# A new order at the head of a long kernel: parameters on another DMA queue, x in four transfers, a split first weight, squares moved back

## The chip, the core and the metric

The kernel runs on one core of a Trainium2 chip. Its time is the device time of one execution in microseconds (us); 1663.65 us is the median of three runs of the kernel before (1662.88 to 1664.98). TensorE (PE) does the matrix products, VectorE (DVE) and ScalarE (ACT) the elementwise work, GpSimd (POOL) almost nothing but small transfers, and SyncE (SP) issues nearly all DMA transfers.

## The reference

Two blocks on 256 tokens of width 1024, all in float32. The first block puts 16 meta tokens in front of x (272 rows) and runs two layers. What the change touches is the head of layer 0:

```
h    = concatenate([meta_tokens, x])                       # 272 x 1024
hn   = h * rsqrt(mean(h*h, axis=-1) + 1e-5) * norm1_g[l]    # first norm
proj = hn @ w_in[l]                                        # 1024 x 2560: q, k, v, u
a, gate = split(u + b_glu[l])
z    = a * sigmoid(gate)                                   # then conv, attention, MLP
```

After the two layers comes a second block: modulated norm, a gated delta rule in chunks, dilated attention, and a mixture of 64 experts of which each token takes 8.

## The kernel before, in words

**Tiling.** Activations lie transposed, 128 of the 1024 features on the partitions and the 272 tokens along the row, so h is eight tiles of 128 x 272. x arrives with tokens on the partitions and is turned by PE: for each of the eight feature blocks three transposes (L320, L322) and one copy out of PSUM by DVE (L323). The meta tokens are in `bigb`, x in `biga`.

**Weights.** A weight tile is 1024 x 256 float32 (1 MB), loaded by `weights` (L158) into one of three buffers `raw`. ACT rounds it in two halves to a high part `hi` (L165), DVE takes the rest as low part `lo` (L166). A product is three matmuls: high by high, high by low of the activations, low by high (L172, L173, L174). The first norm's activations are split in the same way: `xh` by ACT (L268), already times the norm's gain, and `xl` by DVE (L269).

**First norm.** Because the token's scale can be put on afterwards, the products don't wait for it. ACT squares each h tile (L273), PE adds the squares up over the features with a matrix of ones (L274, each in two passes), ACT takes the root (L201) and DVE the reciprocal `rstd` (L202). The results of the first two weight tiles, `a` and `g`, are multiplied by it on the way out of PSUM (L359, L360). Those PSUM tiles are `mm`, of which there are three, and `ax`, also three, one of which holds the sum of squares. The third weight tile needs two more `mm` tiles, so its second half waits until DVE has read the first tile of the first weight, which it can't do before `rstd` is there.

**Parameters.** `columns` (L204) loads rows of parameters and turns them with one transpose into columns. PE does this for norm1_g and b_glu (tile `pv_norm_g`) ahead of all transposes of x.

**What sets the order.** The program is written with tiles and no explicit order between engines; a scheduler works out at build time what stands where in each engine's queue, by a model of the timeline. `high_priority(offset=n)` lets what stands inside count as if it were written n places earlier. Each engine then runs its queue strictly in order. Transfers issued by SP and ACT take eight completion semaphores in turn, and a transfer waits until the earlier holder of its semaphore has landed. POOL issues its own transfers (lam_q, lam_k and other small parameters) with eight of their own; each lam vector is read 128 times, once for each partition.

Of the kernel before, what the change touches and what calls it, by code (L numbers as in the profile page):

```python
# [15 lines left out]
NM, S, D = 16, 256, 1024  # L16
T = NM + S
# [82 lines left out]
def dap(src, off, dims):  # L100
    return bass.AP(tensor=src.tensor, offset=src.offset + off, ap=dims)
# [8 lines left out]
class K:  # L110
    def __init__(s, ctx, tc, I, out, dbg):
        s.ctx, s.tc, s.nc, s.I, s.out, s.dbg = ctx, tc, tc.nc, I, out, dbg
        nc = tc.nc
        s.nraw, s.nhi, s.late = 3, 3, False
        s.V, s.A, s.PE, s.G, s.SP = nc.vector, nc.scalar, nc.tensor, nc.gpsimd, nc.sync
        s.cp = ctx.enter_context(tc.tile_pool(name="cp", bufs=1))
        s.wp = ctx.enter_context(tc.tile_pool(name="wp", bufs=1))
        s.hp = ctx.enter_context(tc.tile_pool(name="hp", bufs=1))
        s.bp_ = [ctx.enter_context(ExitStack()) for _ in range(2)]
        s.bp = [e.enter_context(tc.tile_pool(name="bp" + n, bufs=1, side=n, reuse_waits="tile"))  # L120
                for e, n in zip(s.bp_, ("left", "right"))]
        s.xp = {}
        s.pp_ = ctx.enter_context(ExitStack())
        s.pp = s.pp_.enter_context(tc.tile_pool(name="pp", bufs=1, space=bass.MemoryType.PSUM))
# [28 lines left out]
    def weights(s, src, r0, nk, c0, split=True, ld=None):  # L153

        with s.tc.high_priority(offset=PRI):
            ld = ld or src.ap[-2][0]
            raw = s.wp.tile([128, 8, 256], F32, name="raw", bufs=s.nraw)
            s.SP.dma_start(raw[:, :nk], dap(src, r0 * ld + c0, [[ld, 128], [128 * ld, nk], [1, 256]]))  # L158
            if not split:
                return raw  # L160
            hi = s.wp.tile([128, 8, 256], F32R, name="hi", bufs=s.nhi)
            lo = s.wp.tile([128, 8, 256], F32R, name="lo", bufs=s.nhi)
            h2 = (nk + 1) // 2
            for a, b in ((0, h2), (h2, nk)):
                s.A.copy(hi[:, a:b], raw[:, a:b])  # L165
                s.V.tensor_tensor(lo[:, a:b], raw[:, a:b], hi[:, a:b].bitcast(F32), op=OP.subtract)  # L166
            return hi, lo
# [89 lines left out]
            s.moe()  # L257


    def norm_in(s, h, g, t0, n):  # L260

        ap, A, V = s.ap, s.A, s.V
        xh = ap.tile([128, KC, T], F32R, name="xh")
        xl = ap.tile([128, KC, T], F32R, name="xl")
        ss = s.ax()
        sl = slice(t0, t0 + n)
        for k in range(KC):
            A.activation(xh[:, k, sl], h[:, k, sl], AF.Copy, scale=g[:, k:k + 1])  # L268
            V.scalar_tensor_tensor(xl[:, k, sl], h[:, k, sl], g[:, k:k + 1], xh[:, k, sl].bitcast(F32),  # L269
                                   op0=OP.mult, op1=OP.subtract)  # L270
            sq = ap.tile([128, T], F32, name="sq", bufs=3)
            with s.tc.high_priority(offset=200):
                A.activation(sq[:, :n], h[:, k, sl], AF.Square)  # L273
                s.PE.matmul(ss[:, :n], s.C["ones"], sq[:, :n], start=(k == 0), stop=(k == KC - 1))  # L274
        r = ap.tile([128, T], F32, name="rstd", bufs=2)
        with s.tc.high_priority(offset=200):
            s.rsqrt(r[:, sl], ss[:, :n], s.eps5, 1.0 / D)
        return (xh, xl), r

# [26 lines left out]
    def first_block(s):  # L306
        nc, I, V, A, PE, SP, ap, cp = s.nc, s.I, s.V, s.A, s.PE, s.SP, s.ap, s.cp
        C, ident = dict(s.C), s.C["ident"]
        xin = s.big(0, F32, (2, D))
        xm = s.big(1, F32, (D,))[:NM]  # L310
        with s.tc.high_priority(offset=FIRST):
            for o in range(0, D, D // 2):
                SP.dma_start(xin[:, :, o:o + D // 2], dap(I["x"], o, [[D, 128], [128 * D, 2], [1, D // 2]]))
            SP.dma_start(xm, I["meta_tokens"])
            P = s.columns(ap, ap, (("norm1_g", 16), ("b_glu", 16)), SP, tag="scr", bufs=3)
        h = s.hp.tile([128, KC, T], F32, name="h", bufs=2)
        for k in range(KC):
            p = s.ax()
# [8 lines left out]
        for l in range(2):  # L327
            w_in = I["w_in"][l]
            tq = NM if l else 0
            nq = T - tq  # L330
            x, r = s.norm_in(h, P["norm1_g"][:, 8 * l:8 * l + 8], 0, T)
            if l == 0:
                C.update(s.consts(ap, 1))
                hbg = ap.tile([128, 2, 4], F32, name="hbg")
                for i in range(2):
                    V.tensor_scalar(hbg[:, i], P["b_glu"][:, 8 * i + 4:8 * i + 8], 0.5, None, op0=OP.mult)
            s1 = s.big(0)
# [12 lines left out]
            for b in range(2):  # L350
# [4 lines left out]
                for j in range(2):  # L355
# [5 lines left out]
                    A.activation(g1, g1, AF.Tanh, bias=hbg[:, l, c:c + 1], scale=0.5)  # L361
                    A.activation(a1, a1, AF.Identity, bias=P["b_glu"][:, 8 * l + c:8 * l + c + 1])
                    V.scalar_tensor_tensor(z[:, c, CW - 1:], g1, 1.0, a1, op0=OP.add, op1=OP.mult)
# [6 lines left out]
            for i, (t0, n) in enumerate(((tq, nq), (0, T))):  # L370
# [3 lines left out]
                for b in range(2):  # L374
                    w = s.weights(w_in, 0, 8, 512 * i + 256 * b)
                    for j, p in enumerate(s.block2([(w, 8, 0)], x, t0, n)):
                        raw = ap.tile([128, T], F32, name="qraw", bufs=2)
# [9 lines left out]
            if l == 0:  # L387
                P.update(s.columns(ap, ap, (("norm2_g", 16), ("conv_b", 8), ("conv_ln_g", 8), ("conv_ln_b", 8),
                                            ("subln_g", 2)), s.G, tag="scr", bufs=3))
# [3 lines left out]
                for i in range(2):  # L393
                    V.tensor_scalar(subg[:, i:i + 1], P["subln_g"][:, i:i + 1], 1.0 - LAM0[i], None, op0=OP.mult)
                V.tensor_scalar(hlg, P["conv_ln_g"], 0.5, None, op0=OP.mult)
                V.tensor_scalar(hlb, P["conv_ln_b"], 0.5, None, op0=OP.mult)
# [178 lines left out]
            x, r = s.norm_in(h1, P["norm2_g"][:, 8 * l:8 * l + 8], tq, nq)  # L575
# [17 lines left out]
            h = s.hp.tile([128, KC, T], F32, name="h", bufs=2)  # L593
# [1134 lines left out]
```

## Time and profile before

| | us |
|---|---|
| median of three runs | 1663.65 |
| the profiled execution | 1670.4 |
| its span, first to last instruction | 1668.6 |
| PE busy in the span | 1603.3 |
| DVE busy | 862.3 |
| ACT busy | 757.1 |

The profile is of one execution, 6.75 us longer than the median; 1.8 us of it lie outside the span. "Busy" of PE counts overlapped instructions as well, so 96% is a sign of few gaps, not of a full array. The chain that ended last is 83% PE, 7% DMA (mostly the experts' weights near the end), 5% ACT and 3% DVE. The first 13 us of the span hold no PE instruction at all.

### The profile page before, as it was taken

The numbers are of one execution on the slowest core, as the hardware profiler recorded it, in microseconds if no ns is written. First come the engines' busy times: TensorE is split into PE (matmuls) and PEld (weight loads), VectorE is DVE, ScalarE is ACT, GpSimd is POOL, SyncE is SP. The second block draws the span as 40 slices with busy tenths as digits, with TensorE's granted clock in tenths as the row PEclk, the third lists the DMA queues.
The fourth block names the chain that finished last, engine by engine and source line by source line (L and its number), as shares of the span: only waits on it lengthen the run. The fifth ranks groups of instructions, "written<-read, shape, count | busy, mean of one in ns | idle before, by whom it ended". The sixth has DMA issues, their size and how long they took to land.

```text
span 1668.6 us, 32896 instructions
## 1 busy us (share of the span) xinstructions
PE 1603.3 (96%) x13616; PEld 1358.8 (81%) x13616; DVE 862.3 (52%) x1763; ACT 757.1 (45%) x1548; POOL 14.5 (1%) x28
## 2 busy tenths in 40 slices
PE   6998999999999999998999999999899999999997
PEld 6965999999967999988999899999666576556563
DVE  5685766646986666448655654554322221222122
ACT  5375644435437544455855866743322221222221
POOL 2000000000000000000000000000000000000000
PEclk9999999999988999999999999999999999999999
DMA  8408555555455555653333333556799999999995
GB/s 240 149 26 266 194 179 174 172 178 168 136 177 172 182 189 184 215 191 122 126 128 102 102 128 102 192 192 226 314 380 420 421 419 420 420 419 420 421 419 245
DMA packets 209958, 389.29 MB, mean 233 GB/s; under 512 B 8854, under 2 KB 183312, under 8 KB 184976
## 3 DMA queue, kind: packets, MB, share of 16 engines
q1 hardware_dynamic: 209104, 386.66, 63.1%
q8 instruction: 108, 1.77, 0.4%
q0 software_dynamic: 704, 0.51, 0.3%
q14 instruction: 42, 0.34, 0.1%
HBM read 386.10 MB, written 1.05 MB: 232 GB/s over the span
## 4 chain that ended last, share of the span: by engine, by line
PE 83%; DMA 7%; ACT 5%; DVE 3%; issue 1%; SPq 0%; ACTq 0%; DVEq 0%
PE mm L172 14%; PE mm L174 14%; PE mm L173 14%; PE pm L1542 9%; PE pm L1568 5%; DMA we<-in_w_exp_up 5%; PE pm L1505 3%; PE dx L486 2%; PE mm L195 1%; PE mm L196 1%; PE mm L197 1%; PE dx L628 1%; PE mm L459 1%; PE acc L1586 1%; ACT hi L165 1%; PE ax L274 1%
## 5 line engine op out<-in xcount | busy, mean ns | idle before, releaser
L166 DVE TENSOR_TENSOR lo<-raw,hi 128x1024 fp32r<-128x1024 f32 (+2 forms) x300 | 347.8, 1191 | 144.7 <-ACT hi L165 143.5
L165 ACT CAST hi<-raw 128x1024 fp32r<-128x1024 f32 (+2 forms) x300 | 292.7, 1024 | 267.6 <-PE mm L173 154.0
L172 PE MATMUL mm<-xh,hi 128*128 128x272 f32 (+1 forms) x1008 | 288.1, 288 | 0.0
L173 PE MATMUL mm<-xl,hi 128*128 128x272 f32 (+1 forms) x1008 | 287.8, 286 | 0.0
L174 PE MATMUL mm<-xh,lo 128*128 128x272 f32 (+1 forms) x1008 | 286.6, 286 | 0.0
L1542 PE MATMUL pm<-we,xT 128*32 128x256 f32 (+2 forms) x2048 | 194.2, 389 | 6.3 <-DMA we<-in_w_exp_up 5.5
L173 PEld LDWEIGHTS mm<-xl,hi 128*128 128x128 f32 x1008 | 189.7, 188 | 0.9
L174 PEld LDWEIGHTS mm<-xh,lo 128*128 128x128 f32 x1008 | 189.3, 188 | 0.5
L172 PEld LDWEIGHTS mm<-xh,hi 128*128 128x128 f32 x1008 | 188.5, 188 | 0.8
L1542 PEld LDWEIGHTS pm<-we,xT 128*32 128x32 f32 (+2 forms) x2048 | 123.1, 129 | 72.6 <-DMA we<-in_w_exp_up 7.8
L173 PE MATMUL mm<-bigb,hi 128*128 128x256 f32 (+1 forms) x512 | 148.6, 291 | 0.0
L172 PE MATMUL mm<-hh,hi 128*128 128x256 f32 x384 | 110.5, 291 | 7.3 <-ACT hh L702 4.2
L1568 PE MATMUL pm<-we,hT 128*32 128x512 f32 (+2 forms) x512 | 114.8, 599 | 0.4 <-DMA we<-in_w_exp_down 0.3
L173 PE MATMUL mm<-hl,hi 128*128 128x256 f32 x384 | 109.6, 286 | 0.7 <-DVE hl L703 0.7
L174 PE MATMUL mm<-hh,lo 128*128 128x256 f32 x384 | 108.6, 286 | 0.0
L1553 DVE SCALAR_TENSOR_TENSOR hp<-sil,cs,pm 128x256 f32<-128x256 f32 x26 | 17.6, 676 | 164.8 <-ACT sil L1551 164.8
L174 PE MATMUL mm<-biga,lo 128*128 128x272 f32 (+1 forms) x352 | 101.4, 288 | 0.0
L172 PE MATMUL mm<-biga,hi 128*128 128x272 f32 (+1 forms) x352 | 100.6, 286 | 0.0
L173 PEld LDWEIGHTS mm<-bigb,hi 128*128 128x128 f32 x512 | 97.9, 191 | 0.5
L1573 DVE TENSOR_TENSOR y<-pm,gt 128x512 f32<-128x512 f32 x52 | 35.8, 689 | 107.4 <-PE pm L1568 107.4
L195 PE MATMUL mm<-hi,hh 128*128 128x256 f32 x288 | 86.0, 299 | 2.0 <-DVE cacc L859 2.0
L1551 ACT ACTIVATE sil<-pm 128x256 f32<-128x256 f32 x26 | 10.0, 385 | 170.2 <-PE pm L1542 170.2
(544 smaller groups left out, 3102.7 us busy)
## 6 DMA issues: line engine op xcount, KB each, us to landing
we<-in_w_exp_gate SPq DMA_DIRECT2D x64, 1024.0 KB, 18.2
we<-in_w_exp_up SPq DMA_DIRECT2D x64, 1024.0 KB, 19.5
we<-in_w_exp_down SPq DMA_DIRECT2D x64, 1024.0 KB, 17.7
raw<-in_w_in SPq DMA_DIRECT2D x62, 1024.0 KB, 5.0
raw<-in_w_gate_up SPq DMA_DIRECT2D x44, 1024.0 KB, 5.0
raw<-in_w_ada SPq DMA_DIRECT2D x22, 1024.0 KB, 6.2
raw<-in_w_down SPq DMA_DIRECT2D x16, 1024.0 KB, 5.1
raw<-in_w_out SPq DMA_DIRECT2D x12, 1024.0 KB, 5.4
```

Source lines behind the costliest of these rows:

```text
L165: s.A.copy(hi[:, a:b], raw[:, a:b])
L166: s.V.tensor_tensor(lo[:, a:b], raw[:, a:b], hi[:, a:b].bitcast(F32), op=OP.subtract)
L172: s.PE.matmul(ps[:, :n], a, xh, start=start, stop=False)
L173: s.PE.matmul(ps[:, :n], a, xl, start=False, stop=False)
L174: s.PE.matmul(ps[:, :n], b, xh, start=False, stop=stop)
L195: s.PE.matmul(p[:, :256], xh, w[0][:, k], start=(k == 0), stop=False)
L486: PE.matmul(p[:, :nq], dg, z[:, c, tq + j:tq + j + nq], start=(j == 0), stop=(j == n - 1))
L1505: s.PE.matmul(p[:, 256 * kk:256 * kk + 256], s.ht[h][:, i, k + kk], oh[:, i], start=(i == 0 and h == 0), stop=(i == 1 and h == 1))
L1542: mm = PE.matmul(gu[sg, 256 * m:256 * m + 256], xT[:, k, o + sg.start:o + sg.stop], w[m][:, k], start=(k == 0), stop=(k == 7))
L1553: V.scalar_tensor_tensor(hp.rearrange("p k q -> p q k"), sil.rearrange("p (q k) -> p q k", k=2), cs, gu[:, 256:].rearrange("p (q k) -> p q ...
L1568: PE.matmul(py[sg], hT[:, k, sg], w[2][:, k, 512 * j:512 * j + 512], start=(k == 0), stop=(k == 1))
L1573: V.tensor_tensor(y, py, s.gt2[:, 512 * j:512 * j + 512], op=OP.mult)
```

## The change

It does four things at the head of the kernel. The two transfers of norm1_g and b_glu are issued from ACT's queue and no longer from SP's, and are written ahead of x. x comes in four transfers of 256 columns in place of two of 512, with the meta tokens behind the first of them. The first weight tile comes in two transfers of four row blocks each. In layer 0 the squares, their sums and the reciprocal root get priority offset -200 in place of 200, so they count as written later. Nothing else is edited, but since the scheduler works the whole program out anew, the order changes in later places too, among them the second block.

```diff
-        s.nraw, s.nhi, s.late = 3, 3, False
+        s.nraw, s.nhi, s.late, s.first = 3, 3, False, True
...
-            s.SP.dma_start(raw[:, :nk], dap(src, r0 * ld + c0, [[ld, 128], [128 * ld, nk], [1, 256]]))
+
+            for a, b in ((0, 4), (4, 8)) if s.first else ((0, nk),):
+                s.SP.dma_start(raw[:, a:b], dap(src, (r0 + 128 * a) * ld + c0, [[ld, 128], [128 * ld, b - a], [1, 256]]))
+            s.first = False
...
-    def norm_in(s, h, g, t0, n):
+    def norm_in(s, h, g, t0, n, first=200):
...
-            with s.tc.high_priority(offset=200):
+            with s.tc.high_priority(offset=first):
                 A.activation(sq[:, :n], h[:, k, sl], AF.Square)
                 s.PE.matmul(ss[:, :n], s.C["ones"], sq[:, :n], start=(k == 0), stop=(k == KC - 1))
         r = ap.tile([128, T], F32, name="rstd", bufs=2)
-        with s.tc.high_priority(offset=200):
+        with s.tc.high_priority(offset=first):
             s.rsqrt(r[:, sl], ss[:, :n], s.eps5, 1.0 / D)
...
-            for o in range(0, D, D // 2):
-                SP.dma_start(xin[:, :, o:o + D // 2], dap(I["x"], o, [[D, 128], [128 * D, 2], [1, D // 2]]))
-            SP.dma_start(xm, I["meta_tokens"])
-            P = s.columns(ap, ap, (("norm1_g", 16), ("b_glu", 16)), SP, tag="scr", bufs=3)
+            P = s.columns(ap, ap, (("norm1_g", 16), ("b_glu", 16)), A, tag="scr", bufs=3)
+            for o in range(0, D, D // 4):
+                SP.dma_start(xin[:, :, o:o + D // 4], dap(I["x"], o, [[D, 128], [128 * D, 2], [1, D // 4]]))
+                if o == 0:
+                    SP.dma_start(xm, I["meta_tokens"])
...
-            x, r = s.norm_in(h, P["norm1_g"][:, 8 * l:8 * l + 8], 0, T)
+            x, r = s.norm_in(h, P["norm1_g"][:, 8 * l:8 * l + 8], 0, T, 200 if l else -200)
```

Lines below the edits stand three or four numbers higher in the changed kernel (L274 is L277 there, L172 is L175).

The start of SP's queue, before:

```order
1 L150 DMA blob_73<-in_blob 128x384
2 L313 DMA biga<-in_x 128x2x512 x2
3 L314 DMA bigb<-in_meta_tokens 16x1024
4 L210 DMA pv_norm_g<-in_norm_g 16x128
5 L210 DMA pv_norm_g<-in_b_glu 16x128
6 L158 DMA raw<-in_w_in 128x8x256 x3
7 L150 DMA blob_181<-in_blob 128x944
```

and after (the blob is a table of constants, the identity for the transposes among them):

```order
1 L150 DMA blob_73<-in_blob 128x384
2 L317 DMA biga<-in_x 128x2x256
3 L319 DMA bigb<-in_meta_tokens 16x1024
4 L317 DMA biga<-in_x 128x2x256 x3
5 L160 DMA raw<-in_w_in 128x4x256
6 L160 DMA raw<-in_w_in 128x8x256
7 L160 DMA raw<-in_w_in 128x4x256
8 L160 DMA raw<-in_w_in 128x8x256
9 L150 DMA blob_183<-in_blob 128x944
```

The second half of the first weight has moved behind the second weight, and the two parameter transfers are gone from here; they are the first two rows of ACT's queue now.

PE around the last of the eight sums of squares, with what each row waits for. Before, it lies inside the second weight tile (which writes `ax`), and the first matmul that waits for DVE to free an `mm` tile comes fifty rows later, at row 139:

```order
86 L274 MATMUL ax<-sq,blob_73 128x272 [waits Activation_49]
87 L173 MATMUL ax<-xl,hi 128x272
88 L174 MATMUL ax<-xh,lo 128x272
89 L274 MATMUL ax<-sq,blob_73 128x272 [waits Activation_49]
90 L172 MATMUL ax<-xh,hi 128x272
91 L173 MATMUL ax<-xl,hi 128x272
```

After, it stands at the end of the first half of the third weight tile:

```order
144 L175 MATMUL mm<-xh,hi 128x272
145 L176 MATMUL mm<-xl,hi 128x272
146 L177 MATMUL mm<-xh,lo 128x272
147 L277 MATMUL ax<-sq,blob_73 128x272
148 L175 MATMUL mm<-xh,hi 128x272 [waits DVE_49]
149 L176 MATMUL mm<-xl,hi 128x272
```

The matmul that needs a freed `mm` tile is now the very next one. Between the first weight and row 147 PE does 120 weight matmuls; before row 139 it did 115.

On ACT the root of that norm (L201 before, L204 after) stands behind the high parts of weights four and five, where before it stood between them. The four CASTs ahead of it are these two weights:

```order
18 L168 CAST hi<-raw 128x1024 x3
19 L302 ACTIVATE lsum<-lsum 128x4
20 L168 CAST hi<-raw 128x1024 x4
21 L204 ACT_TABLE_LOAD
22 L204 ACTIVATE rstd<-ax,eps_75 128x272
```

Further down, where the second block's delta rule and dilated attention are interleaved, ACT has 55 table loads in all in place of 51. No edit touches these lines.

## Rows read from the trace of the kernel before

**Rows 1.** The page's head and its engines' busy time.
```profile
span 1668.6 us, 32896 instructions
PE 1603.3 (96%) x13616; PEld 1358.8 (81%) x13616; DVE 862.3 (52%) x1763; ACT 757.1 (45%) x1548; POOL 14.5 (1%) x28
```
**Rows 2.** Waits, first 30 us: who waited for what, us in total, times, longest.
```profile
PE ax L214 <- DMA pv_norm_g<-in_b_glu: 13.1, 1, 13.1
```
**Rows 3.** Timeline of SP's queue (6.54 also alone): start us, duration, what, count.
```profile
0.76 0.39 SPq L150 DMA_DIRECT2D blob<-in_blob  x1
1.20 0.94 SPq L313 DMA_DIRECT2D biga<-in_x  x2
3.15 1.17 SPq L210 DMA_DIRECT2D pv_norm_g<-in_b_glu  x1
4.36 8.65 SPq L158 DMA_DIRECT2D raw<-in_w_in  x3
...
6.54 6.47 SPq L158 DMA_DIRECT2D raw<-in_w_in  x1
...
22.71 0.38 SPq L158 DMA_DIRECT2D raw<-in_w_in  x1
```
**Rows 4.** DMA issues of single stretches: KB each, median us from issue to landing.
```profile
blob<-in_blob SPq DMA_DIRECT2D x1, 192.0 KB, 2.5
pv_norm_g<-in_b_glu SPq DMA_DIRECT2D x1, 8.0 KB, 9.8
raw<-in_w_in SPq DMA_DIRECT2D x1, 1024.0 KB, 11.8
raw<-in_w_in SPq DMA_DIRECT2D x1, 1024.0 KB, 4.9
```
**Rows 5.** The tile views of biga (x) and raw, first 30 us: all landings.
```profile
DMA to landing us min/median/max: 4.8/7.0/9.1
...
DMA to landing us min/median/max: 4.9/9.5/15.7
```
**Rows 6.** Timeline of POOL: its issues held until a lam transfer has landed.
```profile
7.42 0.50 POOL L210 DMA_DIRECT2D pv_norm_g<-in_subln_g  x1 [1.88 <-DMA lamv<-in_lam_q]
13.00 0.51 POOL L210 DMA_DIRECT2D pv_b_ada<-in_g_mix  x1 [0.93 <-DMA lamv<-in_lam_k]
```
**Rows 7.** Timeline of PE: first transposes, squares, first product, third weight.
```profile
13.15 0.26 PE L320 MATMUL ax<-blob,bigb 16*128 16x16 f32 x1
13.96 0.28 PE L320 MATMUL ax<-blob,bigb 16*128 16x16 f32 x1
19.66 2.27 PE L274 MATMUL ax<-sq,blob 128*128 128x272 f32 x6
21.56 0.49 PE L172 MATMUL mm<-xh,hi 128*128 128x272 f32 x1
38.33 0.42 PE L172 MATMUL mm<-xh,hi 128*128 128x272 f32 x2
```
**Rows 8.** The chain of waits, pieces of PE: start, us.
```profile
24.43 0.46 PE ax L274 x2
...
27.39 0.25 PE mm L172 x2
```
**Rows 9.** Timeline of DVE and ACT around weights and the first norm.
```profile
16.96 1.98 ACT L165 CAST hi<-raw 128x1024 fp32r<-128x1024 f32 x2
20.39 2.29 DVE L166 TENSOR_TENSOR lo<-raw,hi 128x1024 fp32r<-128x1024 f32 x2
31.73 1.28 ACT L201 ACT_TABLE_LOAD   x1
33.03 0.49 ACT L201 ACTIVATE rstd<-ax,eps 128x272 f32<-128x272 f32 x1
33.55 1.85 DVE L202 RECIPROCAL rstd<-rstd 128x272 f32<-128x272 f32 x1 [0.39 <-ACT rstd L201]
35.44 0.79 DVE L359 TENSOR_TENSOR a<-mm,rstd 128x272 f32<-128x272 f32 x2
```
**Rows 10.** Windows: us, PE busy, PEld, DVE, ACT, POOL, granted clock, DMA, GB/s.
```profile
30.00:40.00 10.00, 10.00 (x79) 9.84 (x78) 8.66 (x11) 7.33 (x9) 1.34 (x3) 1.00 0.93 290
820.00:845.00 25.00, 24.68 (x247) 23.91 (x246) 18.80 (x41) 22.00 (x56) 1.38 (x1) 1.00 0.36 118
915.00:945.00 30.00, 27.00 (x222) 25.81 (x220) 17.28 (x34) 27.50 (x75) 0.00 (x0) 1.00 0.31 100
```
**Rows 11.** Waits of PE, 915 to 975 us.
```profile
PE dx L1121 <- ACT dpT L1116: 1.7, 1, 1.7
PE dx L1083 <- DVE dtk L1080: 1.3, 1, 1.3
```

## The prediction

> **What bounds the kernel now.** I read the page's head first: PE is busy 1603.3 of 1668.6 us [rows 1], so some 65 us of gaps are all that a change of order can win, and a shift at the head is worth its full length later if PE has no gap behind it. The waits of the first 30 us come next: the longest wait of PE in the whole run is one of 13.1 us for the transfer of b_glu [rows 2]. The reader is to see that this is an 8 KB transfer, issued at 3.15 [rows 3] and landed 9.8 us later [rows 4]. It stood sixth in SP's queue behind all of x. The landings say why the queue is slow: the second half of x was issued at about 1.67 (half of the 0.94 us behind 1.20 [rows 3]) and took 9.1 us, the first half only 4.8 [rows 5]. In the same time POOL's four lam transfers run; the first has landed by 7.42 and the last by 13.00 [rows 6]. I take it that they share the DMA engines with x and that the slowest engine sets when a transfer counts as landed.
>
> From 13.05 PE is a chain: eight blocks of transposes, 0.81 us apart (13.15 to 13.96), squares from 19.66, the first product at 21.56 [rows 7]. From there PE has no gap (10.00 of 10 us in 30 to 40, at granted clock 1.00 [rows 10]). So what counts is when the first products start, and whether PE then runs on.
>
> **The change, part by part.** Its profiled execution took 1670.4 us (span 1668.6 and 1.8 around it), 6.75 more than the median of the runs; I work out differences in that execution and take them off the median.
>
> *Parameters on ACT's queue.* Two issues leave SP's queue and stand first on ACT's, ahead of a table load that nothing needs before h exists. A transfer of 192 KB that is first in its queue lands in 2.5 us [rows 4]; one behind x lands at 13.0. I take the near end, about 3.3, because nothing stands before them now. The cover is x itself: if they land any time before the first quarter of x, they cost nothing.
>
> By the Trainium skill (DMA: Bandwidth & Descriptors, "Issuing engines are not separate DMA queues") transfers started by ScalarE and SyncE run on the same 16 engines and interleave, so that another issuer saves only issue time. Taken at its word, the parameters would land as late as before; that is the slow rival below. That b_glu took four times as long as the 24 times larger constants agrees with a shared engine and with a queue alike; no run so far tells them apart.
>
> *x in four.* Twice the issues (about 0.47 us each, hidden, since the data take longer than the issues). The first quarter lands between 3.3 and the 6.0 of the old half (1.20 + 4.8), I take 4.7. The last lands between 6.0 and the old 10.8 (1.67 + 9.1); of the four lam transfers one now runs ahead of the others, which POOL issues some 2.5 us later, so I take 8.5, the middle. Then two blocks of transposes (1.6) and three sums of squares (1.9, from 19.66 to 21.56 [rows 7]) end at 12.0. Here the transposes are off the path.
>
> *First weight in two.* What is late next is the weights. The first landed at about 16.2 (4.36 + 11.8 [rows 3, 4]), the third at 22.2 (6.54 [rows 3] + the longest landing, 15.7 [rows 5]), so some 3 us a weight. The half weight can land no sooner than 0.5 MB behind x, about 10, and no later than 14.6 (half a step before the old first). Nothing is taken off the DMA engines' work, so I stay near the late end: 13.6, the second weight at 16.7, the second half at 18.3, the third at 21.3. One cast (0.99, half of 1.98 [rows 9]) makes the first product start at 14.7 in place of 21.56. These 6.9 us would be the gain if PE ran on.
>
> *Squares behind the high parts.* This takes much of it back. The last sum of squares is now PE's 147th row, directly ahead of a matmul that needs `rstd`; between them lie the root (0.49), the reciprocal (1.85) and the first product with it (0.44, by the pair's 0.79) [rows 9], 2.8 us in which PE's queue stands. Before, the sum was long done and nothing waited. Two ways lead there:
> - PE's own: 14.7, then 120 products at 0.125 and five sums at 0.46 [rows 8], 15.0 + 2.3, and 1.2 us where the fourth and fifth sum wait for ACT, which squares them behind a cast: 33.2. With the 2.8 us: 36.0.
> - ACT's: its root is now queued behind the casts of weights four and five. The fourth is issued when DVE has the low part of the first weight's second half: landing 18.3, squares and casts ahead on ACT to 20.8, low part 1.15 (half of 2.29 [rows 9]): 22.0, hardly earlier than the 22.71 of before [rows 3]. It lands 4.9 later [rows 4], at 27.0; the fifth, issued with it, at 29.5 to 31.9 (none to one full latency further), I take 29.7. Two casts 1.98, table load 1.28, then the 2.8 us: 35.8.
>
> Before, PE had the same work behind it (115 products at 38.45, five more at 0.125) at 39.1 [rows 7, 8]. So the head gains 39.1 - 36.0 = 3.1 us.
>
> *TensorE's speed.* The first squares came at 0.32 us a pass, later ones at 0.23 [rows 7, 8], though the granted clock of that stretch is not recorded lower. If the first 24 products run at half rate too, they cost up to 3.0 us more; most of that lies in the waits for ACT. I take 0.3, leaving 2.8.
>
> *Later order.* The scheduler's new order brings four more table loads on ACT in the second block, 1.28 each [rows 9]: 5.1 us. ACT is busy 22.00 of 25 and 27.50 of 30 us there [rows 10], but PE waits for ACT or for DVE behind it only now and then (1.7 and 1.3 are the two longest in 60 us [rows 11]). Between 0 and 5.1 I take a quarter, 1.3. That other swaps there gain or lose a microsecond or two can't be read off.
>
> The Trainium skill (ScalarE: Activation LUTs, "What ACT_TABLE_LOAD costs") has 2.66 us for each switch, load and drain; four would be 10.6. The trace shows the root starting 0.02 us behind the load's end (31.73 + 1.28 against 33.03 [rows 9]), so I stay with 1.28.
>
> Sum: -2.8 + 1.3 = -1.5 us, 1663.65 - 1.5 = 1662.1, or 1668.9 for a profiled execution.
>
> **The rivals.**
> - *The weights come much earlier (chance 0.25).* If the lam transfers, later now, no longer hold up the slowest engine, the half weight lands at 10 and the products start at 11. PE's way is then 11 + 18.5 + 2.8 = 32.3; ACT's shifts by the same 3.7 if the low parts keep pace, to 32.1. Gain 6.8, less 0 to 1.3: about 1657.5. For it: the first x half took 4.8 us with one lam transfer in flight. Against it: the same bytes and the same lam transfers still run before 13 us.
> - *The squares come too late for a head that gains little (0.08).* If the parameters land at 13.0 as before, everything up to the first product stays at 21.56, and from there 15.0 + 2.3 + 2.8 make 41.7, which is 2.6 us behind the old 39.1; with the table loads +3.9: 1667.5. The wait of row 148 decides it, and the point is a first product at 17.8: later than that, the head loses. It is the page's rule on issuing engines that would bring this about. Against it: b_glu waited in one queue behind a megabyte.
> - *The table loads all lie on the path (0.12).* +5.1 against -2.8: 1665.9. For it speaks ACT's busy share, against it that PE's named waits there are short.
> - *The transfers gain nothing (0.05).* Four small ones on the same busy engines land as late as two, and the half weight at 14.6 or later: then 1663.5.
>
> **How the numbers follow.** My forecast, 1662.1, has 0.50 with a range of its own from 1659.5 to 1664.5 (weights one microsecond either way, 0 to 3 for the table loads). 0.2% is 3.3 us, about what a measurement of this kernel can tell from no change. Faster than 1660.3 are nearly all of the first rival and a fifth of the forecast: 0.36. Slower than 1667.0 are most of the second rival and part of the third, with swaps in the second block against us: 0.13. The rest, 0.51, is within. The range goes from 1656.5, the first rival without table loads, to 1667.5.
>
> **What would show it.** In the new profile: the transfer of b_glu landing before 5; the first transpose before 6 and the last before 11; the first product between 13 and 16; ACT's root at 32 to 34; and a gap of PE of 2 to 3 us before a product of the third weight, released by DVE's first read of `mm`, at about 36. If PE has no such gap, the squares' price was wrong and the kernel is faster than I say. If the first transpose is still at 13, the queue was not the cause. If the head has gained 3 us at 40 and the end has not, the second block took it, and the two stretches of [rows 10] will show ACT fuller and PE's waits longer.

## The result, and the profile after

The changed kernel takes 1679.95 us (four runs, 1678.99 to 1680.72), the kernel before 1663.27 beside it (four runs, 1662.31 to 1664.98): 1.0099 times as long, 95% interval 1.0081 to 1.0116. That is 16.7 us slower, outside the predicted range. The traced execution took 1680.7 us.

The page's head and its engines' busy time, to be laid beside [rows 1]:

```profile
span 1678.8 us, 32882 instructions
PE 1611.1 (96%) x13616; PEld 1365.4 (81%) x13616; DVE 862.9 (51%) x1763; ACT 762.2 (45%) x1552; POOL 14.5 (1%) x28
```

PE has the same number of matmuls and is busy 7.8 us longer, so part of its work ran slower; the span grew by 10.2, so its gaps grew too. ACT has four instructions more, the four table loads.

PE's waits in the first 50 us (compare [rows 2]), and PE's timeline at the first transpose, the first product, the first product that waits for the root and the products behind it (compare [rows 7]):

```profile
PE ax L217 <- DMA pv_norm_g<-in_b_glu: 4.1, 1, 4.1
PE mm L175 <- DVE a L363: 3.0, 1, 3.0
PE ax L324 <- DMA bigb<-in_meta_tokens: 2.9, 1, 2.9
```
```profile
7.24 0.28 PE L324 MATMUL ax<-blob,bigb 16*128 16x16 f32 x1 [2.86 <-DMA bigb<-in_meta_tokens]
...
13.77 2.27 PE L277 MATMUL ax<-sq,blob 128*128 128x272 f32 x6
15.67 0.49 PE L175 MATMUL mm<-xh,hi 128*128 128x272 f32 x1
16.00 0.29 PE L176 MATMUL mm<-xl,hi 128*128 128x272 f32 x1
16.12 0.29 PE L175 MATMUL mm<-xh,hi 128*128 128x272 f32 x1
...
36.33 0.59 PE L175 MATMUL mm<-xh,hi 128*128 128x272 f32 x1 [2.98 <-DVE a L363]
36.72 0.43 PE L176 MATMUL mm<-xl,hi 128*128 128x272 f32 x1
36.95 0.43 PE L177 MATMUL mm<-xh,lo 128*128 128x272 f32 x1
...
42.59 0.29 PE L175 MATMUL mm<-xh,hi 128*128 128x272 f32 x1
```

ACT's root, DVE's reciprocal and the first read of a product with it (compare [rows 9]):

```profile
33.43 0.49 ACT L204 ACTIVATE rstd<-ax,eps 128x272 f32<-128x272 f32 x1
```
```profile
33.95 1.85 DVE L205 RECIPROCAL rstd<-rstd 128x272 f32<-128x272 f32 x1 [0.38 <-ACT rstd L204]
35.84 0.44 DVE L363 TENSOR_TENSOR a<-mm,rstd 128x272 f32<-128x272 f32 x1
```

Up to here the head's times are near those forecast. Now the windows behind the wait (columns as in [rows 10]; the seventh number behind the window, after POOL, is the granted clock):

```profile
36.00:42.00 6.00, 5.67 (x25) 5.67 (x26) 3.25 (x9) 3.73 (x7) 0.00 (x0) 0.50 0.35 120
42.00:50.00 8.00, 8.00 (x64) 8.00 (x64) 4.24 (x6) 4.07 (x5) 0.00 (x0) 0.97 0.39 133
```

From 36 to 42 us PE had the lower of its two clock levels (1.2 of 2.4 GHz); in [rows 10] the same part of the kernel had 1.00. The 27 products from 36.33 to 42.59 took 6.26 us where 27 times 0.125 are 3.4. That is 2.9 us more, so the 2.8 us that the head had gained were given back there, and behind it the changed kernel stands where the old one stood (row 60 of the table below).

To see where the rest goes, I match the same DVE and ACT instructions of two traces by name and turn, and take the median difference of their starts in stretches of 20 us. All columns are against a second trace of the kernel before (experiment 5), in us; a negative number means that the column's kernel is ahead:

| at | before, 1st trace | after | e1 | e2 | e3 | e4 | e7 | e16 |
|---|---|---|---|---|---|---|---|---|
| 60 | -0.6 | -0.5 | -0.5 | 5.9 | -4.3 | -5.2 | -0.2 | -2.5 |
| 460 | -0.9 | -2.4 | -2.2 | 5.9 | -6.2 | -7.7 | -2.8 | -4.1 |
| 740 | 5.7 | -0.6 | -3.2 | 4.9 | -1.0 | -9.0 | 2.1 | -2.3 |
| 780 | 5.8 | 2.9 | -3.0 | 8.8 | 2.6 | -9.0 | 5.8 | 1.3 |
| 860 | 5.8 | 11.6 | -2.7 | 14.4 | 8.2 | -9.0 | 14.2 | 6.9 |
| 960 | 5.9 | 16.8 | -1.1 | 19.9 | 13.5 | -8.0 | 14.5 | 12.4 |
| 1640 | 5.9 | 16.4 | 0.7 | 19.4 | 13.0 | -6.0 | 16.6 | 11.9 |

The changed kernel loses 17.4 us between 740 and 960, in three places of the second block (740 to 780, 780 to 860, 920 to 960), and nothing behind them. There the scheduler's new order stands.

### The profile page after: what moved, and what is told of

Its sections match the earlier page's. It is cut to its first block, busy times and chain, and to the rows that moved or that the text cites. A ratio compares the mean times of both kernels' runs of the same rounds, so it can differ in the third digit from the quotient of the medians.

```text
span 1678.8 us, 32882 instructions
## 1 busy us (share of the span) xinstructions
PE 1611.1 (96%) x13616; PEld 1365.4 (81%) x13616; DVE 862.9 (51%) x1763; ACT 762.2 (45%) x1552; POOL 14.5 (1%) x28
## 4 chain that ended last, share of the span: by engine, by line
PE 81%; DMA 8%; ACT 6%; DVE 4%; issue 1%; SPq 0%; ACTq 0%; DVEq 0%
PE mm L175 14%; PE mm L176 14%; PE mm L177 14%; PE pm L1546 9%; PE pm L1572 5%; DMA we<-in_w_exp_up 5%; PE pm L1509 2%; PE dx L490 2%; DMA we<-in_w_exp_down 2%; PE mm L198 1%; PE mm L199 1%; PE mm L200 1%; ACT hi L168 1%; PE acc L1590 1%; PE dx L632 1%; PE mm L463 1%
## 5 line engine op out<-in xcount | busy, mean ns | idle before, releaser
L175 PE MATMUL mm<-xh,hi 128*128 128x272 f32 (+1 forms) x1008 | 290.1, 289 | 3.0 <-DVE a L363 3.0
L175 PEld LDWEIGHTS mm<-xh,hi 128*128 128x128 f32 x1008 | 190.1, 189 | 4.1 <-DVE a L363 3.4
L175 PE MATMUL mm<-hh,hi 128*128 128x256 f32 x384 | 111.4, 294 | 9.4 <-ACT hh L706 4.2
L175 PE MATMUL mm<-biga,hi 128*128 128x272 f32 (+1 forms) x352 | 100.6, 286 | 0.0
```

The source lines that it names most:

```text
L175: s.PE.matmul(ps[:, :n], a, xh, start=start, stop=False)
```

## The experiments

For each experiment stand the median time, its ratio to the kernel before as run beside it, and in brackets the 95% interval of that ratio. "Ahead" and "behind" are by starts of the same instructions, as in the table.

**e1: all four edits, old order behind the head.**

```diff
-            x, r = s.norm_in(h, P["norm1_g"][:, 8 * l:8 * l + 8], 0, T, 200 if l else -200)
+            x, r = s.norm_in(h, P["norm1_g"][:, 8 * l:8 * l + 8], 0, T, 200 if l else -100)
```

> All four edits stay, only the squares' offset is -100 in place of -200. The scheduler then keeps the second block in the order of the kernel before (no row of PE behind the head differs, 51 table loads in place of 55), while PE's head differs from the changed kernel's in the place of the last sum of squares alone, 24 products earlier. Theory (the new order of the second block, from 740 to 950 us, brings the loss): about 1663 us, within 3 of the kernel before, and the shift against the trace of before stays between -1 and -7 us from 740 on, where the changed kernel went from -6.4 to +11. Rival (the edits at the head bring it, by the wait for the root and by what follows from it): 1676 to 1681. At the head the wait of PE for the root shrinks from 3.0 us to about 1 (24 products at 0.125 lie behind the last sum now), and if the granted clock then stays at 1.00, the head gains some 5 us and the time is 1658.

1663.51 us, 0.9997 of before (0.9986 to 1.0009). The wait for the root didn't shrink (3.4 us, since the fourth and fifth weight and with them the root came 1.2 us later), and both heads stand level at 60 us in the table. So the pair differs behind the head alone, and the new order costs 1679.95 - 1663.51 = 16.4 us. In the traces 15.3 of it arise between 740 and 960 (from 2.6 to 17.9 between the two columns) and 2.8 between 460 and 740, where the two traces of before differ by more. Whether tiles in PSUM, where PE leaves its sums, also lie elsewhere in the two kernels is not recorded; the order and the tiles' places are not told apart here. PE's longer waits from 725 to 990 us, first of the changed kernel, then of e1 in its shorter stretch 725 to 970:

```profile
PE dx L1087 <- DVE dtk L1084: 3.5, 4, 1.9
PE mm L175 <- DVE cacc L863: 3.5, 2, 3.2
PE ax L953 <- DVE bigb L937: 2.8, 3, 2.1
PE ax L870 <- ACT nsq L868: 2.4, 1, 2.4
...
PE ax L912 <- DVE kdec L839: 1.5, 1, 1.5
```
```profile
PE dx L1087 <- DVE dtk L1084: 2.1, 2, 1.3
...
PE mm L175 <- ACT cacc L860: 0.9, 1, 0.9
PE ax L912 <- DVE bigb L908: 0.8, 1, 0.8
...
PE ax L870 <- ACT nsq L868: 0.6, 1, 0.6
```

The windows of the three places, changed kernel and then e1:

```profile
733.00:800.00 67.00, 56.64 (x432) 53.01 (x432) 49.10 (x87) 37.11 (x67) 0.00 (x0) 0.90 0.44 145
800.00:874.00 74.00, 66.72 (x857) 63.91 (x858) 39.72 (x89) 53.41 (x134) 1.38 (x1) 0.95 0.31 101
924.00:988.00 64.00, 57.66 (x545) 55.66 (x544) 38.78 (x80) 54.03 (x130) 1.38 (x1) 0.92 0.31 100
```
```profile
730.00:790.00 60.00, 52.18 (x413) 48.20 (x412) 47.69 (x84) 36.49 (x64) 0.00 (x0) 0.94 0.49 149
790.00:860.00 70.00, 67.41 (x884) 65.44 (x884) 41.64 (x92) 51.84 (x135) 1.38 (x1) 0.98 0.39 121
910.00:970.00 60.00, 54.71 (x542) 52.35 (x541) 38.31 (x80) 50.90 (x128) 1.38 (x1) 0.97 0.34 107
```

A window's length times what its clock lacks to 1.00 is PE work put off:

| place | table loads, e1, after | named waits of PE, e1, after | put off by the clock, e1, after |
|---|---|---|---|
| first | 3, 3 | 7.7, 10.3 | 3.6, 6.7 |
| second | 10, 12 | 2.6, 7.3 | 1.4, 3.7 |
| third | 10, 12 | 5.3, 6.4 | 1.8, 5.1 |

The waits grew by 8.4 us and the clock's part by 8.7, together 17.1; the three windows grew by 15. The sum is 2 us too large, so the split is rough: about half of the loss is waiting, and about half is low clock. At the first place no table load was added: PE waits 3.2 us, up to 762.3, until DVE has read a PSUM tile (`cacc<-mm`), ahead of which DVE has a weight's low parts:

```profile
759.73 1.22 DVE L169 TENSOR_TENSOR lo<-raw,hi 128x1024 fp32r<-128x1024 f32 x1
760.86 2.82 DVE L863 SCALAR_TENSOR_TENSOR cacc<-mm,gcw,cacc 128x253 f32<-128x253 f32 x7
```

At the second place the longer waits are for DVE; whether they go back to the two added loads was not followed. At the third place the two added loads lie in a chain that PE waits for, though the waits grew by only 1.1 us there, and the clock's part by 3.3. ACT there, changed kernel and then e1:

```profile
948.82 1.28 ACT L204 ACT_TABLE_LOAD   x1
950.12 0.30 ACT L204 ACTIVATE rk<-rk,eps 128x8 f32<-128x8 f32 x1
950.43 1.28 ACT L866 ACT_TABLE_LOAD   x1
951.73 0.42 ACT L866 ACTIVATE bigb<-cacc 128x256 f32<-128x256 f32 x1
952.16 1.28 ACT L204 ACT_TABLE_LOAD   x1
953.46 0.30 ACT L204 ACTIVATE dss<-dss,eps 128x2 f32<-128x2 f32 x1
953.66 0.40 ACT L868 ACTIVATE nsq<-bigb 128x256 f32<-128x256 f32 x1
```
```profile
932.31 0.46 ACT L866 ACTIVATE bigb<-cacc 128x256 f32<-128x256 f32 x1
...
933.12 0.47 ACT L868 ACTIVATE nsq<-bigb 128x256 f32<-128x256 f32 x1
...
934.23 1.28 ACT L204 ACT_TABLE_LOAD   x1
935.52 0.30 ACT L204 ACTIVATE rk<-rk,eps 128x8 f32<-128x8 f32 x1
```

In e1 `bigb` stands ahead of the root; in the changed kernel it lies between two roots, each with its own table, and PE waits 2.42 us for `nsq` behind them.

**e2: the kernel before with the squares at -200 alone.**

```diff
-            x, r = s.norm_in(h, P["norm1_g"][:, 8 * l:8 * l + 8], 0, T)
+            x, r = s.norm_in(h, P["norm1_g"][:, 8 * l:8 * l + 8], 0, T, 200 if l else -200)
```

> The kernel before with the squares' offset -200 as its only edit; x, the weights and the parameters as before. The second block gets the changed kernel's order (55 table loads). Theory (that order costs 10 us or more, and at the head the wait for the root costs its 3 us and a stretch at granted clock 0.50 another 3): first product at 21.6 as before, a gap of about 3 us before a product of the third weight, and 1680 to 1688. Rival (the transfers' edits bring the loss): 1663 to 1669.

1684.24 us, 1.0120 (1.0100 to 1.0139), as the theory had it; only the first product came earlier than it said, at 19.30. There is a wait of 3.4 us for the root up to 42.69, and from 42 to 50 a clock of 0.57; the kernel is 5.9 us behind at 60, and the three places then take another 15.

```profile
42.00:50.00 8.00, 7.31 (x36) 7.31 (x37) 4.63 (x12) 5.36 (x8) 0.00 (x0) 0.57 0.03 9
```

**e3: the other three edits, squares at 200.**

```diff
-            x, r = s.norm_in(h, P["norm1_g"][:, 8 * l:8 * l + 8], 0, T, 200 if l else -200)
+            x, r = s.norm_in(h, P["norm1_g"][:, 8 * l:8 * l + 8], 0, T, 200 if l else 200)
```

> The changed kernel without its last edit: the squares keep the offset 200, the other three edits stay. The second block has the changed kernel's order (55 table loads; 2 rows of PE differ behind the head). Theory (the order of the second block brings the loss): slower still, 1674 to 1680; the head is 3 to 6 us ahead of the kernel before at 50 us, since no wait for the root and no stretch at clock 0.50 remain, and from 740 to 950 us the shift goes up by 15 us or more as in the changed kernel. Rival (putting the squares back is the cause of the loss): 1657 to 1663.

1673.13 us, 1.0055 (1.0036 to 1.0074): 6.8 under the changed kernel and slower than before all the same. The head has no wait and leads by 4.3 at 60; the three places take 14.5 (table). One microsecond under the theory's range.

**e4: parameters on ACT's queue and x in four, nothing else.** The changed kernel with `s.first` false and the squares at 200.

```diff
-        s.nraw, s.nhi, s.late, s.first = 3, 3, False, True
+        s.nraw, s.nhi, s.late, s.first = 3, 3, False, False
```

> Parameters on ACT's queue and x in four transfers; the first weight in one transfer and the squares at offset 200 as before. The second block keeps the order of before but for some 60 rows of PE and 10 of ACT (51 table loads). Theory: the head gains 4 to 6 us (first product between 15 and 19, no wait for the root), nothing is lost later: 1657 to 1661. Rival (a gain at the head is lost in the second block whatever its order): 1663 to 1668. If the loss of the changed kernel comes from the parameters or from x in four, it is 1675 or more.

1659.46 us, 0.9984 (0.9969 to 0.9999): the only version here whose whole interval lies under 1, if barely, and faster than both kernels. The first product stood at 16.80, the granted clock was 1.00 from 30 to 50 us, and the trace is 5.2 us ahead at 60 and 6.0 at the end.

```profile
30.00:50.00 20.00, 20.00 (x162) 20.00 (x161) 12.90 (x24) 10.40 (x16) 0.00 (x0) 1.00 0.64 209
```

**e5: the kernel before, traced again.** No edit.

> The kernel before, unchanged, for a second trace. The traced execution of before took 1670.4 us where its runs had a median near 1663. Theory (that execution met a long stretch at granted clock 0.50 between 490 and 510 us, which the other executions mostly don't have): a span near 1661, some 7 us shorter in the stretch from 470 to 520 and alike within 1 us from 520 to 1000. Rival (the 7 us were spread over the whole run): no stretch of 50 us that differs by over 3 us.

Span 1662.7. The table's first column shows 6.6 us of difference between 460 and 540 and none elsewhere. The first trace and then the second, 490 to 510:

```profile
490.00:510.00 20.00, 19.31 (x111) 12.56 (x112) 9.42 (x31) 10.30 (x29) 1.10 (x2) 0.50 0.75 240
```
```profile
490.00:510.00 20.00, 18.46 (x139) 13.65 (x139) 14.55 (x39) 13.81 (x34) 1.10 (x2) 0.83 1.05 328
```

So the trace on which the prediction rests held 6 us that the second doesn't have, and the difference of the two traced executions (10.3 us) understates the change (16.7).

**e6: the wait for the root filled.** Six products of ones by the last square, read by nothing, behind the last sum.

```diff
+        if first < 0:
+            with s.tc.high_priority(offset=-240):
+                t = s.dx()
+                for i in range(6):
+                    s.PE.matmul(t[:, :n], s.C["ones"], sq[:, :n], start=(i == 0), stop=(i == 6 - 1))
```

> The changed kernel with six more products of PE (ones by the last square, into a PSUM tile that nothing reads) behind the last sum of squares, so that PE works through its wait for the root. All other rows of all engines stand as in the changed kernel, the order of the second block included. Six times 0.46 us are 2.8, a little less than the wait of 3.0. Theory (the wait itself lets the granted clock fall to 0.50, from 35.7 to 42.6 us in the changed kernel): the next product still starts at about 36.3, but the clock stays at 1.00 to 50 us, the head gains 2.9 us and the kernel comes to 1676 to 1678. Rival (the clock falls for another reason, such as the load on DMA or a fixed time after the start): the stretch at 0.50 stays and the time with it, 1679 to 1681.

At the head the theory held: PE waits 0.6 us, the clock stays at 1.00, and the trace is 2.5 us ahead at 60 where the changed kernel is 0.5.

```profile
36.00:42.00 6.00, 5.43 (x42) 5.01 (x41) 4.38 (x11) 3.94 (x7) 0.00 (x0) 1.00 0.50 171
```

The time did not follow: 1682.97, 1.0113 (1.0077 to 1.0148). The trace lost 5.9 us at one place near 1180 (e12 to e16), behind all of the rows that the theory spoke of.

**e7: x in four alone.** To the kernel before:

```diff
-            for o in range(0, D, D // 2):
-                SP.dma_start(xin[:, :, o:o + D // 2], dap(I["x"], o, [[D, 128], [128 * D, 2], [1, D // 2]]))
-            SP.dma_start(xm, I["meta_tokens"])
+            for o in range(0, D, D // 4):
+                SP.dma_start(xin[:, :, o:o + D // 4], dap(I["x"], o, [[D, 128], [128 * D, 2], [1, D // 4]]))
+                if o == 0:
+                    SP.dma_start(xm, I["meta_tokens"])
```

> The kernel before with x in four transfers (the meta tokens behind the first) as its only edit; the parameters stay behind x on SP's queue. Its order is that of the changed kernel at the first two of the three places in the second block and that of before at the third (53 table loads). Theory (each of the three places costs about 5 us by its own rows): up by about 6 at 740 to 800 and by about 5 at 800 to 870, nothing at 915 to 960; the head gains at most 2; 1671 to 1676. Rival (the loss comes with the third place's table loads alone): 1661 to 1665. Rival (any new order there costs the whole): 1678 or more.

1679.85 us, 1.0091 (1.0058 to 1.0124). The places did as the theory said: 3.7 and 8.4 us at the first two (11 expected), 0.3 at the third, where its order is the old one. The time missed it by 4 and lies in the second rival's range: this kernel also lost 4.9 us between 460 and 540, where the two traces of before differ by more; whether it always does there stays open with one trace.

**e8: three edits without the deferral, meta tokens ahead of x.** To the changed kernel:

```diff
+            SP.dma_start(xm, I["meta_tokens"])
...
-                if o == 0:
-                    SP.dma_start(xm, I["meta_tokens"])
...
-            x, r = s.norm_in(h, P["norm1_g"][:, 8 * l:8 * l + 8], 0, T, 200 if l else -200)
+            x, r = s.norm_in(h, P["norm1_g"][:, 8 * l:8 * l + 8], 0, T, 200 if l else 200)
```

> Three of the four edits (parameters on ACT's queue, x in four, the first weight in two), the squares at offset 200 as before, and the meta tokens ahead of the first quarter of x. The second block keeps the order of before (51 table loads) but for some 50 rows of PE. Theory: as good as or better than parameters and x in four without the weight's split (1659.5), since PE's wait of 4.2 us for the meta tokens shrinks to 2 to 3 and nothing else waits: 1655 to 1660, first transpose at about 6, head 5 to 7 us ahead of before at 50 us. Rival (the head's gain isn't limited by the meta tokens but by the first weight): 1659 to 1663.

1662.05 us, 0.9983 (0.9964 to 1.0001), past the expectation though the head leads by 5.0. The first quarter of x itself was what PE then waited for (3.3 us, up to 8.23); from there PE had no gap, and its transposes and sums of squares brought the first product to 16.08. So the rival's time came true and not its reason: PE did not wait for the weight.

**e9: parameters alone.** To the kernel before:

```diff
+            P = s.columns(ap, ap, (("norm1_g", 16), ("b_glu", 16)), A, tag="scr", bufs=3)
...
-            P = s.columns(ap, ap, (("norm1_g", 16), ("b_glu", 16)), SP, tag="scr", bufs=3)
```

> The kernel before with the two parameter transfers on ACT's queue as its only edit; the order behind the head is that of before to the row. Theory: b_glu lands near 4, the first transpose of x starts at about 6 and the last ends with the second half of x, 10.8 to 12; the first product needs the whole first weight (16.2) and its cast, so it starts at 17.5 to 19.5 in place of 21.6; no wait for the root. The head is 2 to 4 us ahead at 50 us and the time 1659.5 to 1661.5. Rival (the parameters were hidden by the weights anyway): the first product at 21 and no change, 1663.

1661.11 us, 0.9986 (0.9972 to 1.0000), in the range. But the first transpose stood at 10.46, not 6: the meta tokens lay behind all of x.

```profile
10.46 0.28 PE L323 MATMUL ax<-blob,bigb 16*128 16x16 f32 x1 [5.87 <-DMA bigb<-in_meta_tokens]
```

**e10: parameters and the weight in two.** To e9:

```diff
-        s.nraw, s.nhi, s.late, s.first = 3, 3, False, False
+        s.nraw, s.nhi, s.late, s.first = 3, 3, False, True
```

> Parameters on ACT's queue and the first weight in two transfers; x in two halves and the squares at 200 as before; the order of the second block as before. Theory: x in four is worth about 1 us at the head, the split of the weight 1 to 2 (first product at 15 to 17): 1658 to 1661, within 1.5 of parameters and x in four. Rival (the split of the weight gives nothing since the second half lands behind the second weight): 1660 to 1663.

1662.45 us, 0.9989 (0.9971 to 1.0008): in the rival's range, but the interval holds 1. The first product stood at 15.95, and the head is 2.1 us ahead at 60, hardly more than with the parameters alone (1.8).

**e11: e4 with the deferral, old order.** To the changed kernel:

```diff
-        s.nraw, s.nhi, s.late, s.first = 3, 3, False, True
+        s.nraw, s.nhi, s.late, s.first = 3, 3, False, False
```

> Parameters on ACT's queue, x in four, the squares at offset -200, the first weight in one transfer: the version of 1659.5 us with the deferral added, and still with the order of before in the second block (51 table loads; 28 rows of PE differ behind the head). It prices the deferral alone. Theory: a wait of about 3 us for the root and a stretch at granted clock 0.50 behind it, worth 3 us more, less what the earlier products gain: +3.5 to +5 against 1659.5, so 1663 to 1665, within 1.5 of before. Rival (the deferral costs its wait of 2.8 at the most, or nothing): 1659.5 to 1662.

1663.43 us, 0.9990 (0.9973 to 1.0006). Against e4 it is 4.0 us, in the range, and 3.2 when each is first compared with the kernel before beside it (-0.4 and -3.6); the two intervals overlap. In the traces it is 5.7 at 60 us. There is a wait of 2.9 us and then the slow stretch:

```profile
35.00:45.00 10.00, 7.06 (x43) 6.59 (x42) 6.50 (x13) 5.88 (x10) 0.00 (x0) 0.83 0.36 115
```

**e12 to e16: does the clock kept at the head arrive at the end?** e12 is e1 with the six products of e6 (offset -200 in place of -240), called dummies below because nothing reads them.

> The version with all four edits, offset -100 and the order of before in the second block (1663.5 us), with the same six products of PE put into the wait for the root; they are the only rows that differ from it. Theory (the wait lets the clock fall, and what the clock keeps at the head arrives at the end): the clock stays at 1.00 from 30 to 50 us, the head gains 2 to 3 us against that version, 1660.5 to 1662. Rival (what is kept at the head is lost again behind 150 us, as half of it was with the changed kernel's order): 1662.5 to 1664.5.

1668.14 us, 1.0030 (1.0016 to 1.0044), slower than both theories. Up to 1160 the trace was 4.5 ahead; then PE waited 7.6 us at 1172. e13 and e14 took two tiles (`for t in (s.dx(), s.dx())`, three products each), e13 on e1, e14 on the changed kernel.

> All four edits, offset -100, the order of before in the second block, and six dummy products of PE in the wait for the root as in the run before, but three each into two PSUM tiles, so that the turn of these tiles later is as without them. Theory (the loss of 5.5 us at 1172 came from the turned tiles, and the clock kept at the head arrives at the end): no wait of 7.6 us at 1172, the clock at 1.00 from 30 to 50 us, 1660 to 1662, some 2 to 3 under the version without dummies (1663.5). Rival (the six products cost what they keep, wherever the tiles lie): 1663 to 1668.

> The changed kernel with six dummy products in the wait for the root, three each into two PSUM tiles; all other rows as in the changed kernel. Theory: the wait of 7.6 us at 1172 is gone, the head keeps 2 to 3 us: 1676 to 1678.5. Rival: 1680 or more.

1667.93 (1.0046, 1.0028 to 1.0063) and 1682.14 (1.0128, 1.0111 to 1.0145): my reason was wrong, the wait of 7.6 us stood in both. e15 and e16 name the `mm` tiles ahead of the first `dx`, so that all PSUM tiles lie as without dummies:

```diff
+            [s.mm() for _ in range(3)]
```

> All four edits, offset -100, the order of before in the second block, six dummy products of PE in the wait for the root, and every PSUM tile at the place that it has without them. Theory (the places brought the wait of 7.6 us at 1172; the clock kept at the head arrives at the end): PE waits 2 us or less at 1172, the clock is 1.00 from 30 to 50 us, 1660 to 1662, against 1663.5 without dummies. Rival (what is kept at the head is lost elsewhere): 1663 to 1665.

> The changed kernel with the six dummy products in the wait for the root and every PSUM tile at its place. Theory: PE waits 2 us or less at 1172 to 1190, the head keeps 2 to 3 us, 1676.5 to 1678.5 against 1680.0. Rival: 1679.5 or more.

The wait, e13 and then e15 (in e16 it is the same 2.0, and without dummies too, in e1 and in the changed kernel):

```profile
PE acc L1307 <- DVE htl L1215: 7.6, 1, 7.6
```
```profile
PE acc L1317 <- ACT gt L1310: 2.0, 1, 2.0
```

e16 takes 1676.14 us (1.0074, 1.0052 to 1.0096), 3.8 under the changed kernel and 6.0 under e14, from which it differs by the tiles named first. By the table it is 2.0 ahead of the changed kernel at 60, 1.6 at 780, 4.7 at 860 and 4.5 at 1640: filling the wait gives 2 us at the head, and the rest arose at the second place, for a reason that was not followed. e15 takes 1663.15 (0.9994, 0.9974 to 1.0013), 0.4 under e1 and in its rival's range, and settles nothing: its executions lie between 1657 and 1671, and its traced one lost 6 us between 460 and 540. So that the clock kept at the head arrives at the end is shown with the new order alone, by one pair of kernels.

## Why the prediction was wrong

**What held.** The parameters landed by 4.1 (below 5 forecast) while x was still on its way. They were also issued earlier, b_glu at 1.20 in place of 3.15; whether the other queue did it or the place ahead of x, no run tells apart. The first product stood at 15.67 (14.7, between 13 and 16), the root at 33.43 (32 to 34), the gap was 2.98 us (2.8) and the product behind it at 36.33 (36.0). The head's 3.1 us were 2.8: 39.1 - 36.33. The lower end of the range holds a slip that changes nothing: 1663.65 - 6.8 is 1656.9 and not 1656.5.

**What held by luck: the first product.** The first transpose came at 7.24 in place of 6, since I had followed x and the weights but not the 64 KB of meta tokens, which landed 5.5 us after their issue. The half weight, on the other hand, landed 7.5 us after its issue at 3.66, at 11.2 in place of 13.6, and its first cast began at 12.42. "Here the transposes are off the path" was therefore wrong: PE had no gap from 7.24 to 15.67, and the transposes (the last from 13.29 on, where I had said before 11) and six sums of squares were what set the first product, not the weight and its cast. Two errors met at about the time forecast. The first rival's half weight at 10 was nearly there, and its gain was not.

```profile
1.20 0.44 ACTq L213 DMA_DIRECT2D pv_norm_g<-in_b_glu  x1
...
12.42 1.03 ACT L168 CAST hi<-raw 128x1024 fp32r<-128x1024 f32 x1
```

**"TensorE's speed", 0.3 us: failed.** The term looked for half rate at the first 24 products, which did not come (16.00 and 16.12 are 0.12 apart). It asked nothing for the products behind the gap: I forecast a gap of nearly 3 us in PE's stream and priced it at its length. In the trace the clock fell to 0.50 within it and 27 products at half rate cost another 2.9, the whole gain of the head. e6 shows that it is the gap: with PE working through it, the clock stays at 1.00. The Trainium skill (TensorE: Matmul & The Clock Gate, "HAM oscillation — how this bites in real kernels") describes a kernel in which PE waits long for a transfer between two bursts of products and starts the next burst at the low clock. The trace agrees in that sequence, with a wait for DVE of 2.98 us and 6.26 us for the products behind it.

**"Later order", 1.3 us: failed, and it is the bulk.** It measured 16.4. I took the four table loads as all that the new order brings, 5.1 us at most, and waved the other moved rows off as a microsecond or two. e1 against the changed kernel shows the bounds were no bounds: 8.4 us of new waits, at the first place without any added load, and 8.7 us of low clock behind them. The evidence for my quarter was that PE's waits in [rows 11] were short, but those were waits of the old order, and neither they nor the two windows of [rows 10] cover the first place (740 to 780), where 3.5 us were lost. My sign for this case was half wrong, too: PE's waits grew, but ACT didn't fill up as I had said: of 30 us around the third place it was busy 25.1 in place of [rows 10]'s 27.5. The window of the changed kernel, with the clock at 0.84 where [rows 10] had 1.00:

```profile
930.00:960.00 30.00, 26.71 (x188) 26.34 (x189) 19.32 (x35) 25.11 (x66) 0.00 (x0) 0.84 0.22 71
```

The sum as measured: -2.8 (head), +2.9 (clock), +16.4 (order) = 16.5, against 16.7. Of the rivals the table loads on the path came nearest in kind and were 14 us short in size; the deferral's price, 2.8 in my second rival, is 3 to 4 by e11 against e4.

**Which edit.** The loss goes with the order and not with any one edit. The squares at -200 alone bring the new order at all three places (1684.24), x in four alone at two (1679.85); the parameters alone (1661.11) and all four edits with -100 (1663.51) keep the old one. The split of the first weight was not run alone. The order's flip is a side effect of the scheduler. With the old order, the head's best version without the deferral (e4) is 3.6 us faster than the kernel before by the medians, 2.7 by the ratio.

## What to carry to other kernels

If a scheduler works the whole program out anew, an edit at the head has two prices, and the larger may lie far behind it, here 0.7 to 0.95 ms: compare the order over the whole program first, and look for a setting that gives the same head with the old order before judging the edit. Price a gap in PE's stream at its length and the slow burst behind it, which here was as much again behind 2.98 us; behind e1's 3.4 us it was 1.8 (a clock of 0.91 from 30 to 50 us). And take a second trace: one execution can hold 6 us that another doesn't.

## What was not expected of the hardware

The clock's response is not a matter of the wait's length alone in these traces: behind the wait of 1.70 us for `dpT` the clock stayed at 1.00 in e1 (915 to 918 us) and fell to 0.50 in the changed kernel (930 to 933). And executions of one and the same kernel spread with it: before ran from 1659.1 us at a mean granted clock of 0.988 to 1674.0 at 0.978, in one series.
